# A decoder trunk on one core: input loaded in its own token order by quarters, first weight split in two steps, low-part products last in the first unit, loads of B behind the second unit's weights

## The chip, the core and the metric

The kernel runs on one core of a Trainium2 chip. The metric is the device time of one execution in microseconds (us). Names of engines: PE is TensorE (PEld its weight load), DVE is VectorE, ACT is ScalarE, POOL is GpSimd, SP is SyncE, which here only issues DMAs.

## What is computed

A trunk of two layers over 256 tokens of width 1024. Each layer adds half a SwiGLU feed-forward block (FFN), a token mixer and another half FFN; the mixer of layer 0 is an S5 state-space layer, that of layer 1 block attention.

```python
def reference(x, ffn_norm, ffn_w_gate, ffn_w_up, ffn_w_down, mix_norm, ...):
    h = x
    for layer in range(2):
        h = h + 0.5 * swiglu(rms_norm(h, ffn_norm[layer, 0]), ffn_w_gate[layer, 0], ffn_w_up[layer, 0], ffn_w_down[layer, 0])
        hn = rms_norm(h, mix_norm[layer])
        h = h + (s5_mixer(hn, ...) if layer == 0 else moba_mixer(hn, ...))
        h = h + 0.5 * swiglu(rms_norm(h, ffn_norm[layer, 1]), ffn_w_gate[layer, 1], ffn_w_up[layer, 1], ffn_w_down[layer, 1])
    return h

def swiglu(h, w_gate, w_up, w_down):          # hidden width 2816
    return (silu(h @ w_gate) * (h @ w_up)) @ w_down
```

`rms_norm` divides each token by its root mean square (one factor per token) and multiplies by a gain per column. The S5 mixer takes matrices `s5_b_*` (B) and `s5_c_*` (C), from which the kernel builds tables.

## The kernel before, in words

**Products.** Everything is float32. A float32 matrix is split into a high part (float32r, rounded) and a low part (the rest, also float32r), and each product of two matrices is three matmuls: high x high, high x low, low x high. In the first FFN these are lines L386, L387 and L388 of the helper `mm3`: 128x128 of the tokens' activations stationary, 128x512 of the weights moving.

**The stream of weights.** Class `Stream` brings in all weights of the trunk in a fixed list of units of 1 MB. `dmas` issues a unit's loads on SP's queue as soon as one of `RAW` = 3 raw buffers is free. `split` makes the two parts of half a unit: ACT writes `whi` (a copy, L81), DVE then writes `wlo = raw - whi` (L82). The parts go into one of `HB` = 9 slots; `release` gives a slot back, and the second split of a unit frees its raw buffer, which at that point of the program issues the loads of the unit three further on. `get` splits whatever is needed and not yet there; `pump` splits ahead, if a slot is free and the unit was issued long enough ago on the kernel's own clock. The program's order is written out by hand: every engine runs its instructions in the order in which the code emits them, so where a `pump` stands decides what stands behind it on ACT and DVE, and a load issued by a split stands on SP behind all DMAs that were emitted before.

**The first FFN** (phase `f00`, function `ffn`) goes by units of 256 hidden columns, j = 0 to 10. The weights of j are two units (`ld_gu`, a = 0 and 1; rows 0 to 511 and 512 to 1023 of `w_gate` and `w_up`), and one unit of `w_down` follows for j - 1. So the list starts: (0,0), (0,1), (1,0), (1,1), `w_down` 0, (2,0), (2,1), `w_down` 1. For j = 0 the loads come in steps of two blocks of rows, four DMAs of 256 KB a unit.

- `gu(j, t)` computes gate and up columns of unit j for token tile t (128 tokens): 8 blocks k of 128 rows, three matmuls each, into PSUM `pM`. `gated` then makes `act`: `sg = silu(r * gate)` on ACT (L468), `act = r * up * sg` on DVE (L472), where r is the token's factor of the norm. `tr` transposes `act` on PE (L485) and splits it into `ah` (ACT, L487) and `al` (DVE, L488). `dn` multiplies by `w_down` and accumulates into the four `psA` banks.
- `gu0` is unit j = 0. The input arrives while it runs, so it goes by quarters q of the rows (blocks 2q and 2q+1), and in each quarter over both token tiles. It accumulates into `psA(0)` and `psA(2)`. At its end stand both gates and then two pumps (the splits of unit 1). The transposes of its `act` stand in the hooks of `gu(1, 0)` at k = 3 and k = 6.

**The input.** `h2` holds the tokens in a permuted order: row s*32 + i of a tile is token 4i + s. `ld_x(n)` loads half n of the columns in four DMAs, one for each s, straight into that order. `ld_x(0)` is issued first of all on SP; `ld_x(1)` is in the list `ahead`, from which `ld_gu` takes it ahead of the second unit's loads. At the end of the main function, `pre` transposes a half of one tile into a `psA` bank (L1320) and multiplies it by the gains in PSUM on DVE (L1321); `parts` splits it into X["h"] (ACT) and X["l"] (DVE); `square` sums squares on ACT. `second` does this for the second half, as the hook (1, 0) of `gu0`, makes both row factors on POOL, and pumps. `busy(n)` issues n matmuls on the tile `ones`, whose results nobody reads (L1333); it is called with 12 and with 6.

**The S5 tables.** `tables` is a generator; `fill` in the first FFN advances it step by step, on DVE, POOL and ACT. `fill(dt)` also moves the kernel's own clock, and `extra` is a list of things due at times of that clock. Loads of B (`ld_b4`, eight DMAs of 64 KB, L729) and of C (`ld_c2`, four) are issued on SP at the steps `LOADS` of the generator.

```python
LOADS, ... = (6, 8, 10, 12, 14, 16, 18, 20, 22, 24, 26, 28), ...     # 8 for B, 4 for C
```

`XO`, `AO` and `OO` are offsets of operands inside larger tiles.

Of the kernel before, what the change touches and what calls it, by code (L numbers as in the profile page):

```python
# [23 lines left out]
HB = 9  # L24
# [8 lines left out]
LOADS, C_AT, E_AT, B_AT, DENSE, LAG, PACE, AGE = (6, 8, 10, 12, 14, 16, 18, 20, 22, 24, 26, 28), 44, 26, 36, 0.46, 12, 4.0, 8.0  # L33


class Stream:


    def __init__(self, nc, units, raw_pool, hl_pool):
# [13 lines left out]
        self.slots = list(range(HB))  # L53
# [18 lines left out]
    def split(self):  # L72
# [7 lines left out]
        if gains is None:  # L80
            nc.scalar.activation(hi, r, AF.Copy)  # L81
            nc.vector.tensor_tensor(lo, r, hi.bitcast(F32), op=OP.subtract)  # L82
# [33 lines left out]
def trunk_kernel(ctx: ExitStack, tc, x, ffn_norm, ffn_w_gate, ffn_w_up, ffn_w_down, mix_norm,  # L116
# [124 lines left out]

    def rows(t, s, n):

        tiles = [[128 * D, 2]] if t is None else []
        return [((t or 0) * 128 + s) * D + n * 512, [[4 * D, 32]] + tiles + [[1, 512]]]

    def ld_x(n):
        for s in range(4):
            off, ap = rows(None, s, n)
            nc.sync.dma_start(h2[s * 32:s * 32 + 32, :, n * 512:(n + 1) * 512],  # L250
                              bass.AP(tensor=x.tensor, offset=x.offset + off, ap=ap))
# [170 lines left out]
    def ffn(tag, nxt, hooks, fill):  # L422
# [23 lines left out]
        def gu0():  # L446
# [3 lines left out]
            for q in range(4):  # L450
                u = us[q // 2]
                for t in range(2):
# [50 lines left out]
        for j in range(NJ):  # L503
            if j == 0:
                gu0()
# [101 lines left out]
    def tables(tp):  # L607
# [22 lines left out]
        for m in MPs + [TT] + t3s:  # L630
            P.memset(m, 0.0)
        yield
        dts = tp.tile([32, 2], F32, name="dts")
        nc.scalar.activation(dts, ldt, AF.Exp)
        dtb = tp.tile([32, 2, 64], F32, name="dtb")
        V.tensor_copy(dtb, dts[:, :, None].to_broadcast([32, 2, 64]))
# [86 lines left out]
        bn = [tp.tile([128, 32, 16], F32, name="bn", tag="n0", bufs=2) for i in range(2)]  # L723
        cn = tp.tile([128, 1280], F32, name="cn", tag="n1", bufs=2)[:, 0:1024].rearrange("p (i a c) -> p i a c", i=2, c=64)
        loads = []

        def ld_b4(i, c):
            b = (s5_b_re, s5_b_im)[i]
            nc.sync.dma_start(bn[i][:, 8 * c:8 * c + 8], bass.AP(tensor=b.tensor, offset=b.offset + 16384 * c,  # L729
                                                                 ap=[[16, 128], [2048, 8], [1, 16]]))  # L730

        def ld_c2(i, a):
            c = (s5_c_re, s5_c_im)[i]
            nc.sync.dma_start(cn[:, i, 4 * a:4 * a + 4], bass.AP(tensor=c.tensor, offset=c.offset + 32768 * a,
                                                                 ap=[[64, 128], [8192, 4], [1, 64]]))

        loads += [lambda i=i, c=c: ld_b4(i, c) for c in range(4) for i in range(2)]
        loads += [lambda i=i, a=a: ld_c2(i, a) for a in range(2) for i in range(2)]
# [553 lines left out]

    tab = tables(tabp) if "s5" in phases else iter(())
    next(tab, None)
    slot = [0]
    extra = [(30.0, more_loads), (50.0, more_gains)]
# [15 lines left out]
    def pre(t, n):  # L1312
# [4 lines left out]
        ps = psA(2 * t + n)  # L1317
        pv = ps.rearrange("p (k c) -> p k c", c=128)
        for k in range(4):
            nc.tensor.transpose(pv[:, k, :], h[t][:, n * 512 + k * 128:n * 512 + (k + 1) * 128], ident)  # L1320
        nc.vector.tensor_tensor(pv, pv, gT[:, n * 4:n * 4 + 4, None].to_broadcast([128, 4, 128]), op=OP.mult)  # L1321
        return pv

    def parts(t, n, pv):
        xh, xl = (X[p][:, n * 4:n * 4 + 4, t * 128:t * 128 + 128] for p in "hl")
        nc.scalar.activation(xh, pv, AF.Copy)
        nc.vector.tensor_tensor(xl, pv, xh.bitcast(F32), op=OP.subtract)
# [7 lines left out]
    busy(12)  # L1335
    gains()
    next(tab, None)
# [96 lines left out]
```

## Time and profile before

| what | value |
|---|---|
| three runs | 1006.88, 1006.81, 1005.18 us; median 1006.81 |
| the profiled execution | 1006.65 us, of which the span from first to last instruction is 1004.8 |
| mean granted clock of TensorE | 0.998 |
| busy time of L386, L387, L388 into pA (first FFN, w_down) | 138.8, 137.7, 137.7 us (352 each) |
| the same three into pM (first FFN, gate and up) | 119.8, 114.0, 113.4 us (288 each) |
| DMA over the span | 197.59 MB, mean 197 GB/s |

How to read it: lines such as L386 are line numbers of the kernel. In a list of groups a row has the line, engine and operation, output and inputs by the program's names, partitions x elements, and xcount; behind the bar the busy time, the mean ns of one, and the idle time of the engine just ahead of such instructions with what ended most of it. In a list in order of time a row begins with the start and the duration in us, and brackets hold the idle time ahead with its releaser. A list of waits has what an engine waited with and for, then the sum, the number of waits and the longest. Matmuls follow each other in a pipeline: the duration of one is longer than the distance to the next.

### The profile page before, as it was taken

What the parts mean: (1) busy time and instruction counts of PE and PEld (TensorE: products, weight loads), DVE (VectorE), ACT (ScalarE), POOL (GpSimd) and SP (SyncE); (2) the same over time, 40 slices, a digit from 0 to 9 for tenths busy, and PEclk for the clock granted to TensorE, in tenths of its full rate; (3) what the DMA queues carried; (4) which work ended last, traced back from release to release, by engine and by line L of the source; (5) the groups of instructions that cost most, each with busy time, mean ns of one, the idle gap of its engine ahead of it and who ended that gap; (6) DMA issues with size and microseconds to landing.
All of it is one profiled execution on the core that took longest, in us unless ns stands there. A gap on an engine that the chain in (4) does not pass through costs nothing.

```text
span 1004.8 us, 16567 instructions
## 1 busy us (share of the span) xinstructions
PE 992.8 (99%) x6394; PEld 889.3 (89%) x6394; DVE 705.2 (70%) x1145; ACT 575.2 (57%) x1040; POOL 166.1 (17%) x330
## 2 busy tenths in 40 slices
PE   8999999999999999999999999999999999999998
PEld 7788888888998999999989999999888899999997
DVE  4799766857977677666657766665689667766662
ACT  5556777754246556555545655553798665555551
POOL 4971222103750100000010000000342010000000
PEclk9999999999999999999999999999999999999999
DMA  8886776886735466565526765655354456756531
GB/s 249 223 292 209 249 260 216 260 317 241 273 115 192 156 220 230 175 203 177 201 85 214 246 207 172 210 168 173 123 163 141 163 167 210 231 189 208 170 126 43
DMA packets 137535, 197.59 MB, mean 197 GB/s; under 512 B 16288, under 2 KB 109040, under 8 KB 137200
## 3 DMA queue, kind: packets, MB, share of 16 engines
q1 hardware_dynamic: 133264, 183.27, 56.6%
q0 software_dynamic: 3616, 12.66, 3.2%
q8 instruction: 50, 0.82, 0.3%
q10 hardware_dynamic: 576, 0.61, 0.2%
q14 instruction: 29, 0.24, 0.1%
HBM read 182.84 MB, written 13.66 MB: 196 GB/s over the span
## 4 chain that ended last, share of the span: by engine, by line
PE 93%; DVE 4%; ACT 1%; issue 1%; POOL 1%; ACTq 0%; POOLq 0%; DVEq 0%
PE pM L541 12%; PE pM L540 12%; PE pM L542 12%; PE pA L387 10%; PE pA L386 10%; PE pA L388 10%; PE pM L387 6%; PE pM L386 6%; PE pM L388 6%; DVE wlo L82 1%; PE pR L322 1%; PE pR L872 1%; PE pR L852 1%; DVE zo L1001 1%; ACT whi L81 1%
## 5 line engine op out<-in xcount | busy, mean ns | idle before, releaser
L540 PE MATMUL pM<-xa,whi 128*128 128x256 f32 x1056 | 295.7, 280 | 0.0
L541 PE MATMUL pM<-xa,whi 128*128 128x256 f32 x1056 | 294.9, 279 | 0.0
L542 PE MATMUL pM<-xa,wlo 128*128 128x256 f32 x1056 | 294.7, 279 | 0.0
L88 DVE SCALAR_TENSOR_TENSOR wlo<-raw,gT,whi 128x512 fp32r<-128x512 f32 x328 | 227.8, 747 | 69.0 <-ACT whi L87 68.9
L82 DVE TENSOR_TENSOR wlo<-raw,whi 128x1024 fp32r<-128x1024 f32 x156 | 191.2, 1241 | 59.6 <-ACT whi L81 58.2
L87 ACT ACTIVATE whi<-raw,gT 128x512 fp32r<-128x512 f32 x328 | 213.4, 711 | 18.0 <-PE pA L388 14.1
L541 PEld LDWEIGHTS pM<-xa,whi 128*128 128x128 f32 x1056 | 198.5, 188 | 2.6
L540 PEld LDWEIGHTS pM<-xa,whi 128*128 128x128 f32 x1056 | 198.5, 188 | 2.3
L542 PEld LDWEIGHTS pM<-xa,wlo 128*128 128x128 f32 x1056 | 198.5, 188 | 0.0
L81 ACT ACTIVATE whi<-raw 128x1024 fp32r<-128x1024 f32 x156 | 160.7, 1054 | 21.1 <-PE pM L541 6.1
L386 PE MATMUL pA<-whi,ah 128*128 128x512 f32 x352 | 138.8, 394 | 0.0
L388 PE MATMUL pA<-whi,al 128*128 128x512 f32 x352 | 137.7, 391 | 0.0
L387 PE MATMUL pA<-wlo,ah 128*128 128x512 f32 x352 | 137.7, 391 | 0.0
L555 ACT ACTIVATE sg<-gr 128x256 f32<-128x256 f32 x66 | 27.6, 418 | 164.7 <-DVE gr L552 164.7
L386 PE MATMUL pM<-whi,xa 128*128 128x512 f32 x288 | 119.8, 416 | 1.5 <-ACT whi L81 1.5
L387 PE MATMUL pM<-wlo,xa 128*128 128x512 f32 x288 | 114.0, 396 | 1.0 <-DVE wlo L82 0.9
L388 PE MATMUL pM<-whi,xa 128*128 128x512 f32 x288 | 113.4, 394 | 0.0
L337 POOL TENSOR_TENSOR ms<-ss 128x1 f32<-128x1 f32 x10 | 1.9, 194 | 474.4 <-ACT sq L334 474.4
L388 PEld LDWEIGHTS pA<-whi,al 128*128 128x128 f32 x352 | 66.1, 188 | 14.3
L386 PEld LDWEIGHTS pA<-whi,ah 128*128 128x128 f32 x352 | 66.2, 188 | 11.6
L387 PEld LDWEIGHTS pA<-wlo,ah 128*128 128x128 f32 x352 | 66.2, 188 | 11.3
L552 DVE TENSOR_TENSOR gr<-pM,rrow 128x512 f32<-128x512 f32 x66 | 45.5, 689 | 39.5 <-PE pM L542 39.4
(253 smaller groups left out, 1283.0 us busy)
## 6 DMA issues: line engine op xcount, KB each, us to landing
raw<-in_ffn_w_down_dram SPq DMA_DIRECT2D x44, 1024.0 KB, 5.4
raw<-in_ffn_w_gate_dram SPq DMA_DIRECT2D x80, 512.0 KB, 4.0
raw<-in_ffn_w_up_dram SPq DMA_DIRECT2D x80, 512.0 KB, 5.1
raw<-in_moba_w_qkv_dram SPq DMA_DIRECT2D x12, 1024.0 KB, 5.2
TB<-dB SPq DMA_DIRECT2D x8, 768.0 KB, 6.2
raw<-in_ffn_w_gate_dram SPq DMA_DIRECT2D x16, 256.0 KB, 4.4
raw<-in_ffn_w_up_dram SPq DMA_DIRECT2D x16, 256.0 KB, 4.6
dB<-tt POOLq DMA_DIRECT2D x16, 256.0 KB, 5.2
```

The source lines that it names most:

```text
L81: nc.scalar.activation(hi, r, AF.Copy)
L82: nc.vector.tensor_tensor(lo, r, hi.bitcast(F32), op=OP.subtract)
L87: nc.scalar.activation(hi[:, c], r[:, c], AF.Identity, scale=g)
L88: nc.vector.scalar_tensor_tensor(lo[:, c], r[:, c], g, hi[:, c].bitcast(F32), op0=OP.mult, op1=OP.subtract)
L386: mm(o, xh, wh, start=start, stop=False)
L387: mm(o, xh, wl, start=False, stop=False)
L388: mm(o, xl, wh, start=False, stop=stop)
L540: mm(o, a, xh, start=k == 0 and i == 0, stop=False, skip_group_check=True)
L541: mm(o, a, xl, start=False, stop=False, skip_group_check=True)
L542: mm(o, b, xh, start=False, stop=k == 7, skip_group_check=True)
L552: V.tensor_tensor(gr, ps.rearrange("p (i c) -> p i c", i=2), Rr["row"][:, None, :].to_broadcast([128, 2, 256]), op=OP.mult)
L555: nc.scalar.activation(sg, gr[:, 0, :], AF.Silu)
```

## The change

1. *The input by quarters, in its own order.* `ld_x(c, n)` loads columns c to c+n of both tiles in natural token order, into two tiles `xn` that lie in the buffers of the ninth slot (the stream starts with eight slots, and `factors` adds the ninth). Columns 0 to 255 are issued first; 256 to 511 go between the second and the third load of weights, and 512 to 1023 after that (`ahead` is now taken at each step k of `ld_gu`, with an empty step first). `quarter(q)` transposes two blocks for both tiles into `psA(1)` and `psA(3)` and writes the output in the permuted order; the gain goes into the splitting instructions themselves as a scale. `h2` is loaded separately by `ld_h`, four DMAs of 256 KB at the kernel's times 54, 60, 66 and 72.
2. *Row factors.* They are computed in natural order and brought into the permuted one by two small transposes, `to_rows` and `to_columns`, in `gu(1, 0)` at k = 1 and 3.
3. *First split in two steps* of 512 columns; all others stay at 1024.
4. *First unit.* In each quarter and tile, `gu0` does high x high for both blocks, low x high for both, and then high x low. It returns its banks; its gates stand in `gu(1, 0)` at k = 4 and 5, its transposes at k = 7 and in `gu(1, 1)` at k = 1. Its hooks hold the pumps, so the splits of unit 1 are emitted ahead of the gates.
5. *Loads of B.* The eight `ld_b4` are the hook (1, 1) of `gu0`. At that place of the program the loads of unit 1 have been emitted and those of `w_down` 0 have not. `LOADS` keeps (22, 24, 26, 28) for C.
6. *Small things.* `busy(12)` and `busy(6)` become `busy(7)` and `busy(3)`; `dtb` is one activation with a broadcast input, without the tile `dts`; `XO['f01']`, `AO` and `OO` fall by 8 elements (32 bytes), and the pool ahead of those tiles grows by 32 bytes.

```diff
-XO = {'f00': 124, 's5': 124, 'g': 0, 'f01': 88, 'f10': 8, 'moba': 124, 'f11': 8}
-AO = (76, 76, 76, 76)
-OO = 76
+XO = {'f00': 124, 's5': 124, 'g': 0, 'f01': 80, 'f10': 8, 'moba': 124, 'f11': 8}
+AO = (68, 68, 68, 68)
+OO = 68
-LOADS, ... = (6, 8, 10, 12, 14, 16, 18, 20, 22, 24, 26, 28), ...
+LOADS, ... = (22, 24, 26, 28), ...
...
-        self.slots = list(range(HB))
+        self.slots = list(range(HB - 1))
...
-            nc.scalar.activation(hi, r, AF.Copy)
-            nc.vector.tensor_tensor(lo, r, hi.bitcast(F32), op=OP.subtract)
+            n = 512 if self.ns == 0 else 1024
+            for a in range(0, 1024, n):
+                c = slice(a, a + n)
+                nc.scalar.activation(hi[:, c], r[:, c], AF.Copy)
+                nc.vector.tensor_tensor(lo[:, c], r[:, c], hi[:, c].bitcast(F32), op=OP.subtract)
...
-            if ahead and a:
-                ahead.pop()()
             for k in range(0, 4, step):
+                if ahead:
+                    ahead.pop(0)()
...
+    xn = [hp.tile([128, D], F32, name="xn", tag=tag, bufs=1) for tag in (f"whi{HB - 1}", f"wlo{HB - 1}")]
+    def ld_x(c, n):
+        for t in range(2):
+            nc.sync.dma_start(xn[t][:, c:c + n], x[0, t * 128:(t + 1) * 128, c:c + n])
+    def ld_h(s):
+        nc.sync.dma_start(h2[s * 32:s * 32 + 32, :, :], bass.AP(tensor=x.tensor, offset=x.offset + s * D,
+                                  ap=[[4 * D, 32], [128 * D, 2], [1, D]]))
...
-    ld_x(0)
+    ld_x(0, 256)
-    ahead.append(lambda: ld_x(1))
+    ahead.extend([lambda: None, lambda: ld_x(256, 256), lambda: ld_x(512, 512)])
...
@@ gu0
-                    for k in (2 * q, 2 * q + 1):
-                        fill(0.7)
-                        wh, wl = st.get(u, q % 2)
-                        c = slice((k % 2) * 512, (k % 2) * 512 + 512)
-                        mm3(pt[t], X["h"][:, k, ts], X["l"][:, k, ts], wh[:, c], wl[:, c], k == 0, k == 7)
+                    fill(1.4)
+                    wh, wl = st.get(u, q % 2)
+                    for i, (part, w) in enumerate((("h", wh), ("l", wh), ("h", wl))):
+                        for k in range(2):
+                            mm(pt[t], X[part][:, 2 * q + k, ts], w[:, k * 512:k * 512 + 512],
+                               start=q + i + k == 0, stop=q + i + k == 6)
                 st.release(u, q % 2)
-            for t in range(2):
-                gated(0, t, pt[t], 0)
-            st.pump(2)
+            return pt
...
-            gu(j, 0, {3: [lambda: tr(0, 0)], 6: [lambda: tr(0, 1)]} if j == 1 else {6: [lambda: tr(j - 1, 1)]})
+            gu(j, 0, {1: [to_rows], 3: [to_columns], 4: [lambda: gated(0, 0, p0[0], 0)], 5: [lambda: gated(0, 1, p0[1], 0)],
+                      7: [lambda: tr(0, 0)]} if j == 1 else {6: [lambda: tr(j - 1, 1)]})
-            gu(j, 1, {6: [lambda: tr(j, 0)]})
+            gu(j, 1, {1: [lambda: tr(0, 1)] if j == 1 else [], 6: [lambda: tr(j, 0)]})
...
@@ tables
+        pre.extend(lambda i=i, c=c: ld_b4(i, c) for c in range(4) for i in range(2))
+        loads = [lambda i=i, a=a: ld_c2(i, a) for a in range(2) for i in range(2)]
...
-    extra = [(30.0, more_loads), (50.0, more_gains)]
+    extra = [(30.0, more_loads), (50.0, more_gains)] + [(54.0 + 6 * s, lambda s=s: ld_h(s)) for s in range(4)]
...
+    def quarter(q, mid=lambda: None):
...
+        pv = [psA(1 + 2 * k)[:, 0:256] for k in range(2)]
+        for k in range(2):
+            for t in range(2):
+                c = (2 * q + k) * 128
+                nc.tensor.transpose(pv[k][:, t * 128:(t + 1) * 128].rearrange("p (s i) -> p i s", s=4),
+                                    xn[t][:, c:c + 128], ident)
+            if k == 0:
+                mid()
+        for k in range(2):
+            g = gT[:, 2 * q + k:2 * q + k + 1]
+            xh, xl = (X[p][:, 2 * q + k, :] for p in "hl")
+            nc.scalar.activation(xh, pv[k], AF.Identity, scale=g)
+            nc.vector.scalar_tensor_tensor(xl, pv[k], g, xh.bitcast(F32), op0=OP.mult, op1=OP.subtract)
...
+    def to_rows():
+        ps = psR()
+        nc.tensor.transpose(ps[0:2, 0:128], rn, ident)
...
+    def to_columns():
+        ps = psR()
+        nc.tensor.transpose(ps[:, 0:2], rT[0], ident[0:2, 0:2])
...
-    pv = [pre(t, 0) for t in range(2)]
-    parts(0, 0, pv[0])
-    next(tab, None)
-    busy(6)
-    st.pump()
-    next(tab, None)
-    parts(1, 0, pv[1])
-    st.pump()
-    for t in range(2):
-        square(t, 0)
-    first = {(1, 0): [second]}
+    busy(7)
+    quarter(0, gains)
+    busy(3)
+    st.pump()
+    next(tab, None)
+    square(0, 0)
+    first = {(0, 1): [st.pump, lambda: next(tab, None), lambda: quarter(1), lambda: square(1, 0)],
+             (1, 0): [lambda: next(tab, None), lambda: quarter(2), st.pump, lambda: square(0, 1)],
+             (1, 1): pre,
+             (2, 0): [lambda: quarter(3), st.pump, lambda: square(1, 1), factors],
+             (3, 0): [st.pump], (3, 1): [st.pump, lambda: warm(AF.Silu)]}
```

More of the change, by code (lines that the diff above doesn't have):

```diff
@@ L240, in trunk_kernel @@
     h = [h2[:, t, :] for t in range(2)]
-    def rows(t, s, n):
[L244 to L251, printed above, removed]
+    xn = [hp.tile([128, D], F32, name="xn", tag=tag, bufs=1) for tag in (f"whi{HB - 1}", f"wlo{HB - 1}")]
[3 more added lines that the diff above has]
+    def ld_h(s):
+        nc.sync.dma_start(h2[s * 32:s * 32 + 32, :, :],
+                          bass.AP(tensor=x.tensor, offset=x.offset + s * D,
+                                  ap=[[4 * D, 32], [128 * D, 2], [1, D]]))
+    def rows(t, s, n):
+        return [(t * 128 + s) * D + n * 512, [[4 * D, 32], [1, 512]]]
     nc.scalar.dma_start(gn, ffn_norm.rearrange("l i (k p) -> (l i k) p", p=128))
-    ld_x(0)
+    ld_x(0, 256)
     warm(AF.Exp)
-    ahead.append(lambda: ld_x(1))
+    ahead.extend([lambda: None, lambda: ld_x(256, 256), lambda: ld_x(512, 512)])
     if "s5" in phases:
@@ L722, in tables @@
         rden = T("rden", 32)
[L723 to L738, printed above, removed]
         def dbl(s_o, c_o, s_i, c_i):
@@ L1290, in moba @@
                     st.release(where["mo", b], i)
+    pre = []
     tab = tables(tabp) if "s5" in phases else iter(())
@@ L1310, in fill @@
             extra.pop(0)[1]()
-    def pre(t, n):
+    def quarter(q, mid=lambda: None):
         if not X:
@@ L1333, in busy @@
             mm(ps[:, 0:128], ones, ones, start=True, stop=True)
-    busy(12)
-    gains()
-    next(tab, None)
     ss4 = sp.tile([128, 2, 2], F32, name="ss4", tag="ss4", bufs=1)
+    v2, rn, r2 = (sp.tile([128, 2], F32, name=n, tag=n, bufs=1) for n in ("ms2", "rn2", "rr2"))
+    rT = []
     def square(t, n):
         sq = sp.tile([128, 512], mybir.dt.bfloat16, name="sq", tag="sq", bufs=1)
-        nc.scalar.activation(sq, h[t][:, n * 512:(n + 1) * 512], AF.Square, accum_out=ss4[:, t, n:n + 1])
@@ L1344, in second, with factors @@
-    def second():
-        pv = [pre(t, 1) for t in range(2)]
-        for t in range(2):
-            parts(t, 1, pv[t])
-        st.pump()
-        for t in range(2):
-            square(t, 1)
-        v2, r2 = (sp.tile([128, 2], F32, name=n, tag=n, bufs=1) for n in ("ms2", "rr2"))
+        nc.scalar.activation(sq, xn[t][:, n * 512:(n + 1) * 512], AF.Square, accum_out=ss4[:, t, n:n + 1])
+    def factors():
         nc.gpsimd.tensor_tensor(v2, ss4[:, :, 0], ss4[:, :, 1], op=OP.add)
         nc.gpsimd.tensor_scalar(v2, v2, 1.0 / D, EPS, op0=OP.mult, op1=OP.add)
-        rsq(r2, v2, 2)
+        rsq(rn, v2, 2)
+        st.slots.append(HB - 1)
@@ L1379, in trunk_kernel @@
             else:
-                ffn(ph, nxt, first, fill)
+                ffn(ph, nxt, first, fill, to_rows, to_columns)
             if i and phases[i - 1] == "s5":
```

36 lines of the change are left out of this document (17 added, 19 removed).

## The prediction

> **What bounds the kernel now.** First the head and engine rows of the page, then PE's waits from 39.3 us to the end.
>
> ```profile
> span 1004.8 us, 16567 instructions
> ...
> PE 992.8 (99%) x6394; PEld 889.3 (89%) x6394; DVE 705.2 (70%) x1145; ACT 575.2 (57%) x1040; POOL 166.1 (17%) x330
> ```
> ```profile
> PE pA L386 <- DVE xa L1085: 1.6, 1, 1.6
> PE pR L1033 <- ACT yg L1039: 0.2, 1, 0.2
> ```
>
> TensorE bounds it. Behind 39.3 us it waits 1.8 us in 965, and the change leaves the matrix products there as they are, so a gain can only come from how early PE gets through the work ahead of that point. The mark for all that follows is the third pair of L485 transposes, at 39.29: tile (j=1, t=0) of the first FFN. The share of 99% hides the start, because the page counts the filler products on `ones` as busy. PE's rows in order of time:
>
> ```profile
> 0.98 5.49 PE L1333 MATMUL pR<-ones 128*128 128x128 f32 x24 [0.98 <-POOL ones L224]
> ...
> 8.00 1.60 PE L1333 MATMUL pR<-ones 128*128 128x128 f32 x12
> 9.99 0.49 PE L386 MATMUL pA<-whi,xa 128*128 128x512 f32 x1 [0.39 <-DVE gm L646]
> 11.30 0.50 PE L387 MATMUL pA<-wlo,xa 128*128 128x512 f32 x1 [0.82 <-DVE wlo L82]
> ...
> 24.28 0.40 PE L388 MATMUL pA<-whi,xa 128*128 128x512 f32 x1
> 26.19 0.50 PE L386 MATMUL pM<-whi,xa 128*128 128x512 f32 x1 [1.51 <-ACT whi L81]
> 27.45 0.80 PE L387 MATMUL pM<-wlo,xa 128*128 128x512 f32 x1 [0.76 <-DVE wlo L82]
> ...
> 32.22 0.39 PE L388 MATMUL pM<-whi,xa 128*128 128x512 f32 x1
> 32.45 0.39 PE L386 MATMUL pM<-whi,xa 128*128 128x512 f32 x1
> ...
> 39.29 0.38 PE L485 MATMUL pR<-cst,act 128*128 128x128 f32 x2
> ```
>
> One 128x512 product takes 0.23 (32.22 to 32.45). Ahead of the mark stand 48 products of j=0 and 42 of j=1: 90 x 0.23 = 20.7 us of real work. PE begins it at 9.99 and reaches the mark 29.3 us later, so 8.6 us are transposes and waits, and the 9 us before are nearly all filler. The largest single piece is at 24.3 to 27.5. Here is why:
>
> ```profile
> 24.72 0.47 ACT L468 ACTIVATE sg<-pA,rr 128x256 f32<-128x256 f32 x1 [0.84 <-PE pA L388]
> 25.09 2.94 ACT L81 ACTIVATE whi<-raw 128x1024 fp32r<-128x1024 f32 x3
> ```
> ```profile
> 23.81:27.22 3.41, 1.37 (x5) 0.56 (x3) 2.02 (x3) 2.57 (x5) 2.81 (x8) 1.00 0.98 257
> 27.23:30.64 3.41, 3.19 (x8) 2.52 (x9) 2.58 (x3) 0.80 (x1) 3.10 (x5) 0.50 0.35 43
> ```
>
> The splits (L81/L82) of the second unit's weights stand on ACT behind the gate `sg` of the first, which waits for all of the first unit's products. The second fence gives windows (length, busy of PE, PEld, DVE, ACT, POOL, then granted clock, DMA share, GB/s): with PE busy 1.37 of 3.41 us, the next 3.41 us are granted half the clock, which costs half of them, 1.7 us.
>
> **The change part by part.** I add durations along the new order of instructions on each engine.
>
> ```profile
> L82 DVE TENSOR_TENSOR wlo<-raw,whi 128x1024 fp32r<-128x1024 f32 x12 | 14.6, 1246 | 3.8 <-ACT whi L81 3.7
> L81 ACT ACTIVATE whi<-raw 128x1024 fp32r<-128x1024 f32 x12 | 12.1, 1048 | 0.0
> ...
> L229 ACT ACT_TABLE_LOAD x2 | 2.6, 1283 | 1.7 <-PEq L1418 1.6
> ...
> L472 DVE SCALAR_TENSOR_TENSOR act<-pA,rr,sg 128x256 f32<-128x256 f32 x2 | 1.0, 484 | 1.7 <-ACT sg L468 1.7
> ...
> L488 DVE TENSOR_TENSOR al<-pR,ah 128x256 fp32r<-128x256 f32 x2 | 0.8, 418 | 1.9 <-ACT ah L487 1.9
> ```
> ```profile
> 4.29 0.47 SPq L170 DMA_DIRECT2D raw<-in_ffn_w_up_dram  x1
> ...
> 13.62 0.51 SPq L170 DMA_DIRECT2D raw<-in_ffn_w_up_dram  x1
> 21.07 0.37 SPq L176 DMA_DIRECT2D raw<-in_ffn_w_down_dram  x1
> ...
> 22.62 3.75 SPq L729 DMA_DIRECT2D bn<-in_s_b_re_dram  x1
> ```
>
> *Quarters of x, filler cut, first split in two.* Filler goes from 18 calls to 10. Two quarter loads of 128 KB each replace four, so the first transposes and the first weights come about a load earlier. The gain factor now enters in the activation itself, and the two L1321 passes go. The new 128x256 forms are not in the trace; I take 0.42 to 0.48 from L488 and L472. What counts is when the second half-unit of weights is there, since quarter 1 and the products of k=2,3 need it:
>
> ```profile
> raw<-in_ffn_w_up_dram SPq DMA_DIRECT2D x1, 256.0 KB, 5.6
> ```
> ```profile
> 8.00:10.00 2.00, 1.61 (x14) 1.42 (x13) 1.93 (x6) 1.54 (x2) 0.00 (x0) 1.00 1.09 241
> 12.00:18.00 6.00, 6.00 (x31) 4.66 (x29) 4.26 (x6) 3.93 (x9) 0.00 (x0) 1.00 1.09 349
> ```
>
> Issued at 4.29 it lands at 9.9, and exactly as many bytes stand ahead of it afterwards (half of x, one unit). The rate was 241 GB/s while 2 KB pieces of x ran and 349 with weights alone. The half of x ahead of it now comes in 1 KB pieces like the weights; 0.5 MB at the higher rate gain 0.7 us, at most 1 with the start. So 8.9 to 9.9.
>
> ```profile
> 9.63 0.25 DVE L643 COPY prm<-pR 128x96 f32<-128x96 f32 x1
> 9.80 0.16 DVE L646 TENSOR_REDUCE gm<-cst 32x2 f32<-32x32 f32 x1
> 9.91 0.19 DVE L615 TENSOR_TENSOR are<-prm 128x32 f32<-128x32 f32 x1
> ```
>
> Then 1.05 (whi), 1.25 (wlo), 0.6 for these three table operations on DVE and 0.45 for the low part of quarter 1, whose PSUM banks quarter 2 needs: PE goes on at 12.2 to 13.2. Behind it 36 products (8.2 us) and nine small transposes (0.11 each, about as the filler calls at 8.00, so 1 us): the first unit ends at 21.4 to 22.4, where it ended at 24.5.
>
> *Low-part products last.* The same 48 products; the wlo wait of 0.8 us in each half is filled with products that need only whi. The low part of x is ready first, so I count no wait.
>
> *Gates of unit 0 put into unit 1.* The splits of unit 1 go ahead of the gates. The 2.3 us of waits (1.51 and 0.76) and the half clock's 1.7 us go. What is late next: ACT's table load (1.28) stands between the second unit's two halves of splits, so PE waits about 0.6 us at k=4. Two transposes for the row factors are added (0.2 us). The first half j=1, t=0 (24 products, 5.5 us) ends at 27.7 to 28.7, and after 18 more products (4.1 us) and a pair of transposes PE is at the mark at 32.1 to 33.1.
>
> *B loads behind the second unit's weights.* Eight B loads now stand on SP's queue ahead of the load of `w_down` 0 (d0). In the program's order d0's first split stands on ACT and DVE ahead of the gate of tile (1,0), which the transposes at the mark read. This is a new wait. How long:
>
> ```profile
> DMA packets 3165, 0.32 MB, mean 114 GB/s; under 512 B 3136, under 2 KB 3136, under 8 KB 3164
> ```
> ```profile
> DMA packets 2115, 0.24 MB, mean 173 GB/s; under 512 B 2087, under 2 KB 2088, under 8 KB 2115
> ```
> ```profile
> raw<-in_ffn_w_up_dram SPq DMA_DIRECT2D x1, 512.0 KB, 7.2
> ```
> ```profile
> raw<-in_ffn_w_down_dram SPq DMA_DIRECT2D x1, 1024.0 KB, 5.7
> ```
>
> The first two fences are the DMA view of 25.3 to 28.1 and of 42.9 to 44.3. A B load is 64 KB in 1024 pieces of 64 B; 3136 pieces in 2.8 us are 0.9 us a load, 2087 in 1.4 us are 0.7. Eight take 5.5 to 7.3 us. The last load of unit 1 lands at 13.62 + 7.2 = 20.8, or a microsecond earlier. With the B loads behind it the queue is through at 25.3 to 28.1, and d0 (1 MB at 349 GB/s, 3.0 us) lands at 28.3 to 31.1 if it follows without a gap. But SP must get past the eighth B load: the third in a row held SP 3.75 us, until the queue had drained to about two B loads. That frees SP at 23.9 to 26.3, and with the 5.7 that d0 took in an empty queue it lands at 29.6 to 32.0. I take 29.6, where the two ranges meet. From the landing: whi 1.05, wlo 1.25, the transposed low part 0.42, second wlo 1.25 (its whi runs beside), the gate product 0.48: 4.4 us. **The mark is at 34.0.**
>
> *The rest.*
>
> ```profile
> 39.29:80.00 40.71, 40.71 (x192) 33.23 (x191) 38.30 (x67) 23.96 (x36) 29.63 (x56) 1.00 0.90 276
> ```
>
> x is loaded once more, 4 x 256 KB in this window. DMA's share is 0.90 (it was 1.09 when full, at 12 to 18), 276 GB/s, and PE is busy throughout: the weights are ahead of it by their buffers. I cost the 1 MB at nothing under that cover; without it, it is 3 us, spread over some 18. The four B loads that ran behind 33 us are gone from there, 2.8 to 3.6 us of DMA. C loads at the same places, `dtb` in one activation and the offsets AO, OO and XO cost nothing: the offsets fall by the 32 bytes by which the pool ahead of those tiles grows, so PE's operands keep their addresses.
>
> **The sum.** 39.29 - 34.0 = 5.3 us off the profiled execution's 1006.65 us (span 1004.8 and 1.85 around it): 1001.35. The median of the three runs is 1006.81, 0.16 more; I forecast 1001.4.
>
> **The rivals.**
> 1. *No wait for d0.* If the B loads cost little, PE's own chain sets the mark at 32.1 to 33.1: 1000.0. Against it: 0.7 us a load at least in both views. By the ceiling of 435 GB/s in the Trainium skill, DMA: Bandwidth & Descriptors, Specifications, the eight would take 1.2 us by bytes alone, an estimate; the rows here say five times that.
> 2. *Half clock in the new wait.* PE idles 1 to 2 us before the mark. Should that fall with other waits into one window as at 23.81, the next window costs 1.7 us: 1003.1. For it: the window rows. Against it: this wait alone leaves over 1.4 of 3.41 us busy. The Trainium skill, TensorE: Matmul & The Clock Gate, Part 1, says the window runs free of the program, and Part 4 that transposes do not count as busy. By that rule the cut filler could also bring the full clock a window later at the start; the work there waits for weights until 12 us, so the sum stays.
> 3. *Given back.* The gain reaches the mark, but later splits or table work run late by as much; within 2 us of before, some 1005.5. For it: DMA's share of 0.90 in the window from 39.29. Against it: no PE wait in that window, and d0's successors follow at 3 us a unit while PE takes 5.5.
> 4. *Slower: SP is held by each B load.* If 3.75 us is the price of every B load from the third on, and not a wait for room, six cost 22.5 us; from 13.6 and a microsecond for the first two, SP is free at 37.1, d0 lands at 42.8, and the mark comes at 47.2: 1014.6. It decides from 2.4 us each (d0 at 34.9). Against it: the 3.75 ended at 26.4, just before the load ahead landed (21.07 + 5.7 = 26.8), as waiting for room would.
>
> **How the numbers follow.** Forecast 0.60, rival 1 0.10, rival 2 0.13, rival 3 0.10, rival 4 0.07. Faster by over 0.2% (2.0 us, about what a measurement can tell from no change): the first three, 0.83; within 0.2%: 0.10; slower: 0.07. The ends of d0 (28.3, with PE's chain as the floor, to 32.0) give 999.5 to 1003.8; with the half clock on part of it the range is 999.3 to 1004.6.
>
> **What would show it.** The first 128x512 product near 7 us; unit 0 through at 21 to 23; splits of unit 1 on ACT before the first `sg`; eight `bn` issues in a row; ACT idle before the fifth unit's `whi`, released by `w_down`'s DMA near 29.6; then the third pair of `cst,act` transposes near 34.0 after 1 to 2 us of PE idle; no PE wait behind it that was not there before. A mark later than 39.3, or new PE waits behind it, would make the forecast wrong.

## The result, and the profile after

The changed kernel takes 1003.57 us (median of 22 runs, 1002.81 to 1006.78) where the kernel before takes 1006.70 (22 runs beside it, 1005.05 to 1008.00). The ratio is 0.9978 with a 95% interval of 0.9972 to 0.9984: 2.2 us faster by the ratio, 3.1 by the medians. Forecast were 1001.4 and a gain of 5.3. The direction and the range held; the size did not.

The runs of either kernel lie 3 to 4 us apart, so two profiles of the changed kernel are shown: first that of an execution of 1005.22, then that of a second one of 1003.44, which is nearer to the median. Line numbers shift with the text of a kernel (`wlo` is L82 before and L85 now, the transposes of `act` L485 and L493). The head and the engine row of the first:

```profile
span 1003.4 us, 16545 instructions
...
PE 991.4 (99%) x6380; PEld 887.4 (88%) x6380; DVE 702.9 (70%) x1147; ACT 576.4 (57%) x1045; POOL 166.5 (17%) x330
```

The shares look as before. What differs is in PE's rows in order of time, and in three windows (length, busy of PE, PEld, DVE, ACT, POOL, granted clock, DMA share, GB/s):

```profile
5.21 0.83 PE L1342 MATMUL pR<-ones 128*128 128x128 f32 x6
7.79 2.17 PE L469 MATMUL pA<-whi,xa 128*128 128x512 f32 x4 [1.75 <-ACT whi L84]
...
35.94 0.38 PE L493 MATMUL pR<-cst,act 128*128 128x128 f32 x2
```
```profile
4.87:8.28 3.41, 1.66 (x10) 1.11 (x9) 1.57 (x4) 2.01 (x5) 3.05 (x6) 1.00 0.93 307
8.28:11.70 3.42, 3.39 (x12) 2.38 (x12) 1.79 (x3) 1.85 (x4) 0.00 (x0) 0.50 1.07 369
11.70:15.11 3.41, 3.41 (x12) 2.72 (x12) 1.57 (x6) 1.75 (x6) 0.00 (x0) 0.50 1.10 350
```

The mark, the third pair of gate transposes, is at 35.94 and not at 34.0. PE lay idle for 1.75 of the first window, and the next two were granted half the clock, just where the first unit's products run. That is this execution's own. The second execution of the same kernel (span 1001.6) has the full clock from 6.86 us on:

```profile
7.15 1.03 PE L469 MATMUL pA<-whi,xa 128*128 128x512 f32 x2 [0.25 <-ACT whi L84]
...
12.38 0.83 PE L1328 MATMUL pA<-cst,xn 128*128 128x128 f32 x4 [1.03 <-DVE xa L1336]
...
22.06 0.39 PE L395 MATMUL pM<-whi,xa 128*128 128x512 f32 x1
...
24.77 0.50 PE L396 MATMUL pM<-wlo,xa 128*128 128x512 f32 x1 [0.83 <-DVE wlo L85]
...
34.00 0.44 PE L493 MATMUL pR<-cst,act 128*128 128x128 f32 x2
...
52.53 0.44 PE L493 MATMUL pR<-cst,act 128*128 128x128 f32 x2 [1.37 <-DVE act L480]
```

Here the mark is at 34.00, the forecast place: 5.29 us before the 39.29 of the kernel before. Yet its span is only 3.2 us shorter than the 1004.8 of before. The missing 2 us go behind the mark. Product 132 of the first FFN (128x512 products counted from 0, in PE's order) starts at 44.14 instead of 49.35, still 5.21 early; product 216 starts at 68.20 instead of 71.04, only 2.84 early. PE's list of waits from 30 us to the end has two rows between the two that the kernel before does not have:

```profile
PE pR L493 <- DVE act L480: 1.4, 1, 1.4
PE pR L293 <- DVE al L496: 0.4, 1, 0.4
```

Both wait for DVE. DVE's rows in order of time, first of the kernel before, then of this execution, say what held it:

```profile
46.47 0.19 DVE L678 COPY e<-c 128x16 f32<-128x16 f32 x1
```
```profile
23.28 0.35 DVE L772 RECIPROCAL rden<-den 128x32 f32<-128x32 f32 x1 [2.36 <-POOL den L684]
23.55 1.16 DVE L85 TENSOR_TENSOR wlo<-raw,whi 128x1024 fp32r<-128x1024 f32 x1
...
24.82 1.20 DVE L85 TENSOR_TENSOR wlo<-raw,whi 128x1024 fp32r<-128x1024 f32 x1
...
26.02 1.20 DVE L85 TENSOR_TENSOR wlo<-raw,whi 128x1024 fp32r<-128x1024 f32 x1
...
45.48 0.22 DVE L699 COPY e<-c 128x16 f32<-128x16 f32 x1 [3.88 <-POOL c L690]
...
52.00 0.47 DVE L480 SCALAR_TENSOR_TENSOR act<-pM,rr,sg 128x256 f32<-128x256 f32 x1
```

The copy of `c` is the first table instruction on DVE that needs the end of POOL's long chain of table work. In the kernel before DVE came to it at 46.47 without a wait. Now DVE comes 4.9 us earlier, stands still for 3.88, and the splits and the gate behind it in its queue are late: the gate `act` at 52.00 is what PE waits 1.37 for. POOL's rows before (with DVE's `wlo` of that time), then in this execution:

```profile
18.91 0.19 POOL L1353 TENSOR_TENSOR ms<-ss 128x2 f32<-128x2 f32 x1 [10.94 <-ACT sq L1342]
...
22.95 0.23 POOL L669 TENSOR_SCALAR q<-aim 128x32 f32<-128x32 f32 x1
23.26 0.31 POOL L667 TENSOR_SCALAR q<-q 128x32 f32<-128x32 f32 x1
...
26.18 1.31 POOL L663 TENSOR_TENSOR y<-y 128x32 f32<-128x32 f32 x1
...
42.26 0.22 POOL L669 TENSOR_SCALAR c<-e 128x32 f32<-128x32 f32 x1
```
```profile
26.17 3.64 DVE L82 TENSOR_TENSOR wlo<-raw,whi 128x1024 fp32r<-128x1024 f32 x3 [0.46 <-ACT whi L81]
```
```profile
18.70 0.62 POOL L1353 TENSOR_TENSOR ms<-ss 128x2 f32<-128x2 f32 x1 [10.20 <-ACT sq L1350]
...
23.55 1.24 POOL L690 TENSOR_SCALAR q<-aim 128x32 f32<-128x32 f32 x1
24.87 2.52 POOL L688 TENSOR_SCALAR q<-q 128x32 f32<-128x32 f32 x1
...
45.23 0.21 POOL L690 TENSOR_SCALAR c<-e 128x32 f32<-128x32 f32 x1
```

POOL begins the row factors (and then the chain) at 18.7, as before, lies idle for 10 us ahead of it, and gets to `c` at 45.45 instead of 42.48. In the kernel before this left 46.47 - 42.48 = 4.0 us of slack that no list of waits shows. PE's lead took up 4.9, and the chain's own delay 3.0: 4.0 - 4.9 - 3.0 = -3.9, the 3.88 of the row. The delay comes from single instructions: `q<-q` took 0.31 before and 2.52 now, and its 24.87 to 27.39 lies over the two `wlo` from 24.82 to 27.22. The splits of unit 1 are not the whole of it. In the kernel before three of them stood over the same chain, only a little later in it (26.17 to 29.81, `y<-y` took 1.31). Of the 48 instructions from `ms` to `c`, 8 took over 0.9 us before (9.5 us together), and 10 now (14.1). So what grew is the number of `wlo` that lie over the chain: 9 before, 12 now. The Trainium skill, SBUF — State Buffer, Who interferes with whom, says that a DVE instruction with two SBUF inputs (`wlo` has two) contends with a GpSimd instruction that reads SBUF, and that the ports they share are an exclusive lock. If the lock is held for one whole instruction, a 0.3 us instruction on POOL becomes about as long as the `wlo` beside it: `q<-aim` agrees (1.24 beside a `wlo` of 1.16), while `q<-q` waited through two `wlo` in a row.

### The profile page after: what moved, and what is told of

Its sections match the earlier page's. It is cut to its first block, busy times and chain, and to the rows that moved or that the text cites. A ratio compares the mean times of both kernels' runs of the same rounds, so it can differ in the third digit from the quotient of the medians.

```text
span 1003.4 us, 16545 instructions
## 1 busy us (share of the span) xinstructions
PE 991.4 (99%) x6380; PEld 887.4 (88%) x6380; DVE 702.9 (70%) x1147; ACT 576.4 (57%) x1045; POOL 166.5 (17%) x330
## 4 chain that ended last, share of the span: by engine, by line
PE 84%; DVE 5%; POOL 5%; issue 3%; ACT 1%; DMA 1%; SPq 0%; POOLq 0%; ACTq 0%; DVEq 0%
PE pM L550 12%; PE pM L549 12%; PE pM L551 12%; PE pA L395 9%; PE pA L397 9%; PE pA L396 9%; PE pM L395 4%; PE pM L396 4%; PE pM L397 4%; DVE wlo L85 1%; POOL sc L684 1%; POOL qrs L304 1%; PE pR L331 1%; PE pA L469 1%; PE pR L878 1%
## 5 line engine op out<-in xcount | busy, mean ns | idle before, releaser
L85 DVE TENSOR_TENSOR wlo<-raw,whi 128x1024 fp32r<-128x1024 f32 (+1 forms) x157 | 191.7, 1235 | 59.5 <-ACT whi L84 58.6
L84 ACT ACTIVATE whi<-raw 128x1024 fp32r<-128x1024 f32 (+1 forms) x157 | 160.7, 1048 | 25.9 <-PE pA L397 6.8
```

The lines of the kernel that those rows point to most:

```text
L84: nc.scalar.activation(hi[:, c], r[:, c], AF.Copy)
L85: nc.vector.tensor_tensor(lo[:, c], r[:, c], hi[:, c].bitcast(F32), op=OP.subtract)
```

## The experiments

The first column of times is the median, the second the ratio to the kernel before on the same chip, then the mark and the span in the profile. The mark varies between executions (the cut chain alone has it at 33.63 and at 33.97). Rows 1 to 4 ran on one chip, and so did 5 to 8, 9 to 11 and 12 to 14.

| run | us | ratio, 95% | mark | span |
|---|---|---|---|---|
| changed kernel again | 1003.67 | 0.9981 (0.9972 to 0.9990) | 34.00 | 1001.6 |
| more filler | 1003.46 | 0.9980 (0.9971 to 0.9989) | 34.47 | 1001.7 |
| POOL's chain cut | 1001.01 | 0.9958 (0.9946 to 0.9971) | 33.63 | 998.9 |
| B loads back | 1003.24 | 0.9982 (0.9972 to 0.9991) | 33.93 | 1001.4 |
| before + gates | 1003.44 | 0.9977 (0.9968 to 0.9986) | 34.53 | 1001.2 |
| before + gates + chain cut | 1002.30 | 0.9966 (0.9953 to 0.9978) | 34.47 | 1000.5 |
| chain cut, low part inline | 1000.79 | 0.9958 (0.9943 to 0.9974) | 33.52 | 998.8 |
| chain cut, one first split | 1001.77 | 0.9962 (0.9948 to 0.9976) | 34.25 | 999.5 |
| changed, tables later | 1002.40 | 0.9973 (0.9962 to 0.9983) | 33.76 | 1000.4 |
| before + chain cut | 1005.15 | 0.9998 (0.9989 to 1.0007) | 39.23 | 1004.7 |
| chain cut, B back, rows later | 1004.16 | 0.9983 (0.9973 to 0.9993) | 33.65 | 1002.8 |
| chain cut, rows later | 1001.97 | 0.9962 (0.9949 to 0.9974) | 34.37 | 1000.2 |
| chain cut, B back | 1001.06 | 0.9956 (0.9942 to 0.9970) | 33.17 | 999.1 |
| chain cut again | 1001.72 | 0.9960 (0.9947 to 0.9972) | 33.97 | 1000.8 |

**The changed kernel once more** (no edit).

> The changed kernel once more, for a second profile. Theory A (the gain is lost in two places: the half clock that is granted from 8.28 to 15.11 us, right behind a window in which PE lay idle from 6.04 to 7.79, and POOL's chain of table work, which begins at 20.98 where it began at 18.91 and which DVE waits for at 25.5 and 47.3): a profile that shows the full clock from 8 to 15 us has the third pair of transposes near 33.5 to 34.5 instead of 35.94, and the waits of PE behind it (1.4 us at 53.0) grow, to 2 or 3 us, because POOL's chain does not come earlier; the span is then 1001 to 1002. If the same windows are halved again, all places are as before within 0.3. Rival B (the DMAs ahead of d0 set everything): the third pair stays at 35.5 to 36.5 whatever the clock, since d0 lands at 30.2.

The full clock, the mark at 34.00, the span 1001.6. Theory A holds on the mark and the span; it missed on the wait, which stayed at 1.37 and did not grow, because POOL's chain also came 1.8 us earlier when the start ran at the full clock (`c` ended at 45.45; in the other profile at 47.29). So what the half clock cost in the first profile stayed to the end: 1.94 at the mark, 1.8 in the span.

**More filler.**

```diff
-    busy(3)
+    busy(11)
```

> Eight more filler calls behind the first quarter's transposes (11 instead of 3, 16 matmuls of 0.11 us, about the 1.75 us that PE lay idle). Theory A: no half clock between 8 and 15 us, the third pair of transposes at 33.5 to 34.5, but part of it given back behind it at POOL's chain: 0.5 to 2 us faster than the changed kernel. Rival B (DMAs ahead of d0): no difference within 0.5 us. Rival C (filler holds PE up): 0.5 to 1 us slower.

Nothing: 1003.46 against 1003.67 on the same chip. The full clock is there with and without it. Another run below (one first split) has nearly as much idle time in its first window and is not halved behind it:

```profile
4.99:8.40 3.41, 1.74 (x12) 1.46 (x12) 1.76 (x4) 2.62 (x6) 3.37 (x6) 1.00 1.02 337
8.40:11.82 3.42, 3.36 (x18) 2.08 (x16) 1.92 (x4) 2.54 (x6) 0.60 (x1) 1.00 1.07 367
```

So the cut filler does not by itself bring the half clock, and what does is open; one profile of two of this kernel shows it.

**POOL's chain cut in two.**

```diff
         pt(y2, y, y, OP.mult)
+        yield
...
-             (2, 0): [lambda: quarter(3), ...
+             (2, 0): [lambda: next(tab, None), lambda: quarter(3), ...
```

> POOL's table chain is cut in two steps, and its first 14 instructions are put ahead of the row factors, where POOL lies idle from about 13 to 21 us. Theory A: DVE's waits for POOL at 25.5 (2.35 us) and at 43.5 (3.86 us) go, with them PE's waits of 0.82 at 26.2 and 1.39 at 53.0: 1.5 to 2.5 us faster than the changed kernel, near 1001.3. Rival B (the wait at 53 is late weights, behind the B loads): no more than 0.8 us faster (the first wait alone), the 1.39 stays. Rival C (the row factors are made late by the table work ahead of them): slower, with a new PE wait at the small transposes of the row factors.

On the same chip 2.7 us faster than the changed kernel by the medians and 2.3 by the ratios, whose intervals do not overlap (the repeat below has 0.9960). PE's waits from 13 us to the end, POOL's `q` and `c`, and DVE's copy of `c`:

```profile
PE pA L395 <- DVE xa L1092: 1.6, 1, 1.6
PE pR L1362 <- POOL rn L308: 0.6, 1, 0.6
PE pR L493 <- DVE act L480: 0.3, 1, 0.3
```
```profile
13.12 0.31 POOL L688 TENSOR_SCALAR q<-q 128x32 f32<-128x32 f32 x1
...
38.51 1.29 POOL L690 TENSOR_SCALAR c<-e 128x32 f32<-128x32 f32 x1
```
```profile
40.84 0.18 DVE L699 COPY e<-c 128x16 f32<-128x16 f32 x1
```

`q<-q` runs at 13.12, in what was idle time, in 0.31 again; `c` is there at 39.80, and DVE takes it without a wait. The 0.83 at 24.8 and the 1.37 at 52.5 are gone, as theory A had it. The lead now stays to the end: product 132 starts at 43.78 and product 216 at 65.47, each 5.57 earlier than before the change, and the span is 6.0 shorter. Rival C shows a little: the row factors come late by 0.55.

**The loads of B back behind d0.**

```diff
-LOADS, ... = (22, 24, 26, 28), ...
+LOADS, ... = (6, 8, 10, 12, 14, 16, 18, 20, 22, 24, 26, 28), ...
-        pre.extend(lambda i=i, c=c: ld_b4(i, c) for c in range(4) for i in range(2))
-        loads = [lambda i=i, a=a: ld_c2(i, a) ...]
+        loads = [lambda i=i, c=c: ld_b4(i, c) for c in range(4) for i in range(2)]
+        loads += [lambda i=i, a=a: ld_c2(i, a) ...]
```

> The changed kernel with the eight loads of B back at steps 6 to 20 of the table generator, behind d0. Theory A: d0 lands well before 28, but PE reaches the third pair of transposes when it did, 35.9 within 0.3 (at the same clock), and the end stays within 0.7 us of the changed kernel: the B loads cost nothing where they stand, and moving them gained nothing. Rival B (the loads ahead of d0 hold the gain back): 1.5 to 2.5 us faster than the changed kernel. Rival D (the move of the B loads is what brought the gain, by freeing the queue later): 1 to 2 us slower.

1003.24 against 1003.67, the mark at 33.93 without a wait for d0 (which lands at 25.6): theory A, for this kernel. Whether that hid behind POOL's chain was asked again below.

**The gates alone, on the kernel before.**

```diff
-            for t in range(2):
-                gated(0, t, pt[t], 0)
             st.pump(2)
+            return pt
...
-            gu(j, 0, {3: [lambda: tr(0, 0)], 6: [lambda: tr(0, 1)]} if j == 1 ...
+            gu(j, 0, {4: [lambda: gated(0, 0, p0[0], 0)], 5: [lambda: gated(0, 1, p0[1], 0)],
+                      7: [lambda: tr(0, 0)]} if j == 1 ...
-            gu(j, 1, {6: [lambda: tr(j, 0)]})
+            gu(j, 1, {1: [lambda: tr(0, 1)] if j == 1 else [], 6: [lambda: tr(j, 0)]})
```

> The kernel before with one part of the change alone: the gates of unit 0 and their transposes are put into unit 1 (k = 4, 5, 7 of tile 0 and k = 1 of tile 1), behind the splits of unit 1. Theory A: PE's waits of 1.51 and 0.76 at 25 to 27.5 go, and with them the half clock behind them (1.7): the third pair of transposes at 35.0 to 36.0 instead of 39.29. The end gains less, since DVE then reaches its first table instruction that needs POOL's chain when that chain ends, or earlier: 2 to 4 us faster than before, 1002.7 to 1004.7, about as the whole change. Rival B (the quarters of the input and the cut filler bring the gain): less than 1.5 us faster.

1003.44: this one part gives the whole time of the change. ACT now has the splits ahead of the gates, and PE is at the mark at 34.53, 4.76 early; rows of ACT and PE:

```profile
22.12 2.94 ACT L81 ACTIVATE whi<-raw 128x1024 fp32r<-128x1024 f32 x3
24.97 0.81 ACT L467 ACTIVATE sg<-pA,rr 128x256 f32<-128x256 f32 x2
```
```profile
34.53 0.38 PE L484 MATMUL pR<-cst,act 128*128 128x128 f32 x2
```

Here too DVE then waits for POOL, 2.43 us at 44.7, and PE for DVE:

```profile
44.72 0.22 DVE L678 COPY e<-c 128x16 f32<-128x16 f32 x1 [2.43 <-POOL c L669]
```
```profile
PE pR L284 <- DVE al L487: 0.5, 1, 0.5
PE pR L484 <- DVE act L471: 0.3, 1, 0.3
```

**The gates and the cut chain, on the kernel before** (as above, with the `yield`, and a `next(tab, None)` at the head of `second`).

> The same, and POOL's table chain cut in two, its first 14 instructions ahead of the row factors, as in the run with the whole change. Theory A: whatever the chain took back is there at the end: the whole 3.3 to 4.3 us of the third pair, near 1002.5, and no wait of PE for the gates of the third unit. Rival B (the chain matters only with the whole change): no difference to the gates alone within 0.5 us.

1002.30: 1.1 less than the gates alone, as theory A had it. The intervals of the two ratios overlap, but PE's waits of 0.5 and 0.3 are gone, and product 216 starts at 66.83 instead of 67.57. What the rest of the change is worth can be read only here, with POOL out of the way: 1002.30 against 1001.01 and 1001.72, 0.6 to 1.3 us by the medians and 0.6 to 0.8 by the ratios, which is not clear of the noise, with the spans 1000.5 against 998.9 and 1000.8 (this last one with a half clock of 3.4 us at 307).

**Each block's three products together again** (chain cut; `mm3` in `gu0` as before the change).

> The changed kernel with POOL's chain cut in two, and in the first unit each block's three products together again (high x low second), as before the change. Theory A: each of the first two splits' low parts is waited for again (0.4 to 0.8 us each in the trace of before), but the products behind wait for the input's second quarter anyway; the third pair of transposes 0.2 to 1.0 later than with low-part products last, the end likewise: 1001.2 to 1002.0. Rival B (the order does nothing): within 0.2 us.

1000.79 and the mark at 33.52: no difference to be seen, rival B. The order of the low-part products is worth nothing here; PE waits for the input's second quarter in either order.

**The first split in one step** (chain cut; `n = 1024`).

> The changed kernel with POOL's chain cut in two, and the first split in one step of 1024 columns. Theory A: the first product comes 0.4 to 0.5 us later (1.05 for the whole copy on ACT against 0.63 for its first half), and that is swallowed by PE's wait for the second quarter of the input at 12.3: no difference at the third pair or the end within 0.3 us. Rival B: 0.4 to 0.6 us slower throughout.

1001.77, the mark at 34.25 with 0.76 of waiting for d0, which landed at 29.87 (29.26 in the run that it is compared with). The first product starts at 7.73 against 7.71 (7.50 in the repeat), so the 0.4 to 0.5 us that theory A began with cannot be seen. Beside the repeat of the cut chain (1001.72) there is no difference, as theory A had it for the end.

**DVE's table instructions later.**

```diff
-..., C_AT, E_AT, ... = ..., 44, 26, ...
+..., C_AT, E_AT, ... = ..., 44, 31, ...
```

> The changed kernel with one number changed: the first of DVE's table instructions that need POOL's chain may start at 31 of the kernel's clock instead of 26, three splits and a gate further down in DVE's order. POOL's chain stays as it is. Theory A (the gain is lost because DVE, standing at such an instruction, holds up the splits and the gate behind it): PE's wait of 1.37 at 52.5 goes, and most of the loss between 44 and 70 us with it: 1.0 to 2.0 us faster than the changed kernel, 1001.6 to 1002.6. Rival B (POOL's chain itself, or DVE's total load, is the limit): the same loss a little later, within 0.5 us of the changed kernel.

1002.40. By the ratios that is 0.8 us faster than the changed kernel, which ran on another chip, and the intervals overlap; so the profile has to say it. Its span is 1.2 less than that of the changed kernel's second profile, with POOL's chain untouched (`c` at 47.97, even later). DVE now has the splits, `al` and `act` ahead of the table work, and PE's wait at 52.5 is gone. One new wait at 64.3 keeps the rest, so each theory holds in part: the place in DVE's queue was the cause of the wait at 52.5, and the table work that was moved still has to be done.

```profile
45.20 0.41 DVE L496 TENSOR_TENSOR al<-pR,ah 128x256 fp32r<-128x256 f32 x1
45.54 0.47 DVE L480 SCALAR_TENSOR_TENSOR act<-pM,rr,sg 128x256 f32<-128x256 f32 x1
45.97 0.07 DVE L697 MEMSET e<- 128x16 f32 x1
...
48.00 0.22 DVE L699 COPY e<-c 128x16 f32<-128x16 f32 x1 [1.93 <-POOL c L690]
```
```profile
PE pR L818 <- DVE al L496: 1.4, 1, 1.4
```

**The cut chain alone, on the kernel before.**

> The kernel before with POOL's chain cut in two and nothing else. Theory A: the kernel before had room there (POOL's chain ended at 42.5, DVE needed it at 46.5), so the end stays: within 0.5 us of before. Rival B (the chain cost time in the kernel before as well, and the run with the whole change gained from that, not from what the change had lost): 1 us or more faster than before.

Ratio 0.9998: nothing. The chain was slack in the kernel before and became the limit through the change, theory A.

**Cut chain, B loads back, and the first small transpose at k = 2** (`{1: [to_rows]` becomes `{2: [to_rows]`).

> The changed kernel with POOL's chain cut in two, the loads of B back behind d0, and the first small transpose of the row factors at k = 2 instead of 1. Theory A: the wait for the row factors (0.55 at 23.3) and that for d0's splits (0.29 at the third pair) go: 0.3 to 0.9 us faster than with the chain cut alone, 1000.1 to 1000.7. Rival B (transfers of B in a later window hold up weights): no faster, 1001 or more.

A miss: 1004.16 (12 runs, 1001.97 to 1006.34). In the profile the mark is early (33.65), and 2 us are lost at one place. Another 1.7 of its span are a half clock of 3.41 us at 309.

```profile
65.09 0.63 PE L819 MATMUL pR<-cst,cn 128*64 128x128 f32 x4 [1.84 <-DVE al L496]
```

Its two edits were then run apart, beside the cut chain alone.

> The changed kernel with POOL's chain cut in two and the first small transpose of the row factors at k = 2 instead of 1; the loads of B stay ahead of d0. Theory A (the B loads put back were the loss): PE's wait of 0.55 for the row factors goes and the loss is not there: 0.2 to 0.6 us faster than with the chain cut alone, 1000.4 to 1000.9. Rival B (the moved transpose was the loss): 2 us slower, with a wait of 1.8 near 65.

> The changed kernel with POOL's chain cut in two and the loads of B back behind d0, the transpose where the change has it. Theory A: the weights that land at 54.7 with the B loads ahead land near 57, DVE's splits are late behind them, PE waits 1.5 to 2 us near 65, and the end is 2 to 3 us slower than with the chain cut alone: 1003 to 1004. Rival B: no such wait, within 0.5 us of 1001.

> The changed kernel with POOL's chain cut in two and nothing else, once more, so that the other two have it on their own chip: 1000.6 to 1001.4 as before.

Neither edit alone is the loss. The transpose at k = 2 alone gives 1001.97 beside 1001.72: not faster, since its successor then waits 0.56 for DVE's copy. The B loads back alone give 1001.06, with the mark at 33.17: rival B, and the 2 to 3 us of theory A are not there. Nor is a lead left. PE is 0.46 ahead of the first run of the cut chain at 59.53, and 0.11 behind it at 60.32, where it waits for ACT's copies of C (`cb`). These stand behind a split whose weights land 2 us later with the B loads back. ACT's rows with the B loads ahead, then ACT's and PE's with them back:

```profile
54.78 2.01 ACT L84 ACTIVATE whi<-raw 128x1024 fp32r<-128x1024 f32 x2 [0.89 <-DMA raw<-in_ffn_w_up_dram]
```
```profile
56.81 2.01 ACT L84 ACTIVATE whi<-raw 128x1024 fp32r<-128x1024 f32 x2 [1.32 <-DMA raw<-in_ffn_w_up_dram]
58.73 1.54 ACT L822 ACTIVATE cb<-pR 64x256 f32<-64x256 f32 x4
```
```profile
60.32 0.63 PE L819 MATMUL pR<-cst,cn 128*64 128x128 f32 x4 [0.35 <-ACT cb L822]
```

So the late weights of theory A are there (near 57), and cost PE 0.35 instead of 1.5 to 2. In the miss the two edits meet. With the transpose at k = 2 alone the last transposes of C wait 0.51 for `al` on DVE, at 64.11. With the B loads back alone `al` runs later, at 64.51, but the same transposes do not wait for it, at 62.86. With both they wait, and `al` is late (64.63): 1.84. Why they wait for `al` in one order and not in the other is open. They write one of two `pR` buffers, and another buffer would explain it, but no run shows that.

## Why the prediction was right or wrong

- *The bound and the mark.* TensorE does bound it. The mark came at 34.00 as forecast, in part by luck. Forecast were d0's landing and 4.4 us, with PE idle for 1 to 2 us before. d0's side came out so, but PE's own work was through only at 33.85, and with the B loads back, where nothing waits for d0, the mark is at 33.93 all the same. And only until PE's wait at 51 was the mark worth what the sum said.
- *Quarters, filler, first split.* The first unit ended at 22.06 (forecast 21.4 to 22.4), and PE went on with the second quarter at 12.4 (12.2 to 13.2). But little of the gain at the mark comes from there: the gates alone give 4.76 of 5.29. The whole change begins the second unit 2.4 us earlier than the gates alone (22.06 against 24.48) and reaches the mark only 0.5 earlier (34.00 against 34.53).
- *Low-part products last.* No wait counted, none seen; worth nothing either.
- *Gates.* The mechanism is right: waits and half clock go. The size was 4.0 (2.3 and 1.7) and measured 4.76 in the profiles. The half clock's 1.7 was taken from one execution, and not every execution of the kernel before seems to have it. Of its 27 runs on one chip ten had a mean granted clock of 0.999 or 1.0 and took 1005.0 to 1005.3; the others had 0.998 or less and took 1006.2 or more, as the profiled one did. Taken from all, the 1.7 is too much; this would be why the gain is 3.1 by the medians and 2.2 by the ratio.
- *The wait at k = 4.* Forecast 0.6 from ACT's table load, measured 0.83, with another cause: `rden` on DVE waited 2.36 for POOL, and `wlo` stood behind it. That was the first sight of what ate the gain.
- *B loads ahead of d0.* In the second profile ACT's first split of d0 starts at 29.59, against a landing forecast at 29.6. SP was held 2.88 and 2.56 by the second and third load and 0.6 to 1.8 by the later ones, so rival 4 falls. PE waited 0.15 for it and not 1 to 2 us, since its own chain came at 33.85 and not at 32.1 to 33.1. ACT's rows of that profile:

```profile
26.13 0.84 ACT L476 ACTIVATE sg<-pA,rr 128x256 f32<-128x256 f32 x2 [2.20 <-DVE rr L1368]
29.59 1.06 ACT L84 ACTIVATE whi<-raw 128x1024 fp32r<-128x1024 f32 x1 [2.62 <-DMA raw<-in_ffn_w_down_dram]
```

- *The rest, and rival 3.* **This is the step that failed.** The prediction took the gain at the mark to the end because the weights were ahead of PE and because PE had no wait in the window from 39.29. Rival 3 named the right thing, later splits or table work that run late by as much, and was given 0.10. An empty list of waits says that nothing is late now; it does not say by how much. The slack was 4.0 us at the copy of `c`, to be read from two rows of the profile of before, and the change itself also slowed the chain by 3.0. 2.4 of 5.3 us went there, and with the chain cut none did.
- *Rival 2.* The half clock did come in one profile, at the start and not in the new wait. "The work there waits for weights until 12 us, so the sum stays" was wrong for that execution: 1.94 at the mark.

## What to carry to other kernels

Before a gain on the critical engine is carried to the end, look for each place behind it where another engine's long chain meets the queue, and read its slack: when the producer ends, and when the consumer comes to it. What is moved beside such a chain can lengthen it as well. And of a change of many parts, try the one that removes the largest wait alone: here the order of gates and splits gave the whole time, and a cut in the chain that the rest laid bare gave nearly as much again.

## What the runs showed of the hardware

A 128x32 instruction on POOL takes 0.2 to 0.3 us alone and 1.1 to 1.3 beside one 128x1024 `wlo` on DVE; one that met two `wlo` in a row took 2.52. The three `wlo` from 23.55 to 27.22 took 1.16 to 1.20. Where a short POOL instruction was already under way, later `wlo` of that profile took up to 1.38, against 1.23 with POOL idle.

The first window at the full clock began at 4.87 us in one execution of the changed kernel and at 6.86 in the other. After nearly the same share of busy PE in the first window at the full clock, one execution kept it (1.74 of 3.41 us) and another was granted half of it for the next 6.8 us (1.66 of 3.41). In two executions of the cut chain PE was busy 1.79 of 3.41 us in a window near 303; one kept the full clock, the other was granted half of it for 3.41 us. So the busy share alone does not tell which it will be.
